# Input tiles of another layout between the first weight loads, and a quarter of the last norm's columns on GpSimd, in a two-layer decoder trunk

## The chip, the cores and the metric

The kernel runs on one core of a Trainium2 chip. A core has a matrix engine (TensorE, PE in the profile; its weight loads are PEld), VectorE (DVE), ScalarE (ACT), GpSimd (POOL) and SyncE (SP), which here issues most DMAs. The metric is the device time of one execution in microseconds (us), as the median of several runs.

## The reference

Two layers of a decoder trunk on 256 tokens of 1024 channels, all in 32-bit floats. Each layer is a half-step SwiGLU with a layer norm, three token mixers (gated DeltaNet, sliding-window attention, cross-attention to a memory) whose outputs are gated and projected, a layer norm, and a second half-step SwiGLU with a layer norm:

```python
def hybrid_layer(x, ...):
    h = layer_norm(ALPHA * x + 0.5 * swiglu(x, ffn1_w_gu, ffn1_w_down), ln_g[0], ln_b[0])
    ...
    h = layer_norm(ALPHA * h + merged @ w_out, ln_g[1], ln_b[1])
    return layer_norm(ALPHA * h + 0.5 * swiglu(h, ffn2_w_gu, ffn2_w_down), ln_g[2], ln_b[2])
```

What matters here is the first product, `x @ ffn1_w_gu` of layer 0, with which the kernel starts, and the last layer norm of layer 1, with which it ends.

## The kernel before

**Products.** A 32-bit factor is split into a high part, rounded to the matrix engine's reduced type, and a low part, the rest. `split` (line 121) does this with one cast on ACT and one subtraction on DVE. A product is then three matmuls (`mm3`): high by high, high by low, low by high.

**Weights.** All weights lie in DRAM in one stream `wst`, in the order of use. `unit` (lines 104 to 119) takes the next piece, normally 128 partitions by 1024 columns (512 KB): SP loads it into a tile `raw` (4 buffers), `split` makes `whi` and `wlo` (5 buffers each). With `cuts=2` it does so in two halves of 512 columns, each with its own DMA, cast and subtraction.

**The start.** The input is needed with channels on partitions. `xT` in DRAM is the plain transpose, 1024 channels by 256 tokens; `xload` (line 1047) loads 256 channels of it as a tile `t` of 128 partitions by 2 rows of 256 tokens (1 KB each, 256 KB in all), and splits it into `hT`. `Ffn.__init__` calls `xload(q)` and `unit` in turn for q = 0 to 3, the first unit in halves. So four x tiles and four weight units alternate on SP's queue; then follow the constants `cs` (488 KB, with the identity matrix for the transposes) and the further weights. `Ffn.both` (line 328) multiplies: for each k of 128 channels and each of two blocks of 128 tokens three matmuls of 512 columns, 48 in all, 12 for each weight unit. PE's order is fixed by the scheduler when the kernel is built; at the first k of a whole unit it places the two products with `whi` of both token blocks ahead of the first with `wlo`.

**The rest.** Then come the other gate and up columns, the down projection, the mixers and so on, for two layers. SP's queue keeps its order; a weight load waits until its `raw` buffer is free. DMAs from SP use eight completion semaphores in turn, so each waits for the one eight places ahead.

**The end.** The last down projection is ordered so that token block 1 ends last, its last 512 columns in two pieces of 256. `Post.__call__` calls `layernorm` (line 263) for each token block: add the residual (line 409), statistics (272, 275), the root on ACT (279), its reciprocal with one correction step on DVE (280 to 283), and for each half c of 512 columns two operations on DVE: `(y - mean) * g` (286) and `y * rs + b` (287). `fin` stores each half with a DMA from SP (416). GpSimd does nothing in this stretch.

Of the kernel before, what the change touches and what calls it, by code (L numbers as in the profile page):

```python
# [14 lines left out]
ALU = mybir.AluOpType  # L15
AX = mybir.AxisListType

P = 128
D = 1024
S = 256  # L20
# [3 lines left out]
KD = D // P  # L24
# [14 lines left out]
def tile_trunk(ctx, tc, x, xT, mem, memT_, wst, lnp, memln, cvw, rows, cst, out):  # L39
# [36 lines left out]
    def load(dst, src):  # L76

        tc.keep_in_program_order(nc.sync.dma_start(dst, src))
# [22 lines left out]

    pos, newest = [0], []

    def unit(w=U, dst=None, cuts=1, behind=None):
        ahead = tc.high_priority(offset=AHEAD) if pos[0] >= 8 * P * U else nullcontext()
        raw = T(praw, [P, U], "raw")
        src = wst[pos[0]:pos[0] + P * w].rearrange("(p w) -> p w", p=P)
        pos[0] += P * w
        (ph, th), (pl, tl) = dst or ((phi, "whi"), (plo, "wlo"))
        with ahead:  # L110
            hi = T(ph, [P, U], th, F32R)
            lo = T(pl, [P, U], tl, F32R)
            for i in range(cuts):
                c = slice(i * w // cuts, (i + 1) * w // cuts)
                nc.sync.dma_start(raw[:, c], src[:, c])
                with tc.issue_after(behind) if behind else nullcontext():
                    newest[:] = split(hi[:, c], lo[:, c], raw[:, c])
        return hi, lo
# [141 lines left out]
            nc.vector.tensor_tensor(t, t, v, op=ALU.mult)  # L260
            nc.vector.scalar_tensor_tensor(y, t, 1.5, y, op0=ALU.add, op1=ALU.mult)

    def layernorm(y, gB, bB, eps, src=None, fin=None, sizes=(512, 512)):
        n = min(sizes)
        st = T(p3, [P, 4, 6], "bnst")[:, :D // n, :]
        done = at_ = 0
        for j, size in enumerate(sizes):
            if src:
                src(j, slice(at_, at_ + size))
            at_ += size  # L270
            while done < at_:
                nc.vector.bn_stats(st[:, done // n, :], y[:, done:done + n])
                done += n
        mv = T(p3, [P, 2], "bnmv")
        nc.vector.bn_aggr(mv, st)
        rs = T(p3, [P, 1], "rstd")
        rt = T(p3, [P, 1], "rst")

        nc.scalar.activation(rs, mv[:, 1:2], AF.Sqrt, bias=epsc[:, eps:eps + 1])
        nc.vector.reciprocal(rs, rs)  # L280
        nc.vector.scalar_tensor_tensor(rt, mv[:, 1:2], epsc[:, eps:eps + 1], rs, op0=ALU.add, op1=ALU.mult)
        nc.vector.scalar_tensor_tensor(rt, rt, -0.5, rs, op0=ALU.mult, op1=ALU.mult)
        nc.vector.scalar_tensor_tensor(rs, rt, 1.5, rs, op0=ALU.add, op1=ALU.mult)
        for c in range(2):
            cc = slice(c * 512, (c + 1) * 512)
            nc.vector.scalar_tensor_tensor(y[:, cc], y[:, cc], mv[:, 0:1], gB[:, cc], op0=ALU.subtract, op1=ALU.mult)
            ins = nc.vector.scalar_tensor_tensor(y[:, cc], y[:, cc], rs, bB[:, cc], op0=ALU.mult, op1=ALU.add)
            if fin:
                fin(c)
        return ins.ins  # L290
# [9 lines left out]
    class Ffn:  # L300
        def __init__(self, before=None):
            self.units = []
            for q in range(KD // 2):
                if before:
                    before(q)
                self.units.append(unit(cuts=2 if before and q == 0 else 1))
            self.hu, self.bank, self.due = {}, {}, []

        def h(self, i):
# [76 lines left out]
    class Post:  # L386
# [12 lines left out]
        def __call__(self, tb, outs):  # L399
            if tb == 0:  # L400
                self.gb = gb(*self.aps)
                self.hT = None if self.last else new_hT()
            y = hres[tb]

            def put(q):
                return self.hT[0][:, q * 4:q * 4 + 4, :], self.hT[1][:, q * 4:q * 4 + 4, :]

            def src(j, c):
                nc.vector.scalar_tensor_tensor(y[:, c], outs[tb][j], 0.5 / ALPHA, y[:, c], op0=ALU.mult, op1=ALU.add)

            turns = []

            def fin(c):
                if self.last:
                    cc = slice(c * 512, (c + 1) * 512)
                    nc.sync.dma_start(out[tb * P:(tb + 1) * P, cc], y[:, cc])
                elif tb == 0:

                    turns.append(lambda: to_T(put, tb, y, c))
                else:  # L420
                    to_T(put, tb, y, c)

            self.end = layernorm(y, *self.gb, 1, src, fin, [o.shape[-1] for o in outs[tb]])
            return turns

    def begin(nxt, hT):
# [615 lines left out]


    hT = new_hT()
    xv = xT.rearrange("(k p) t -> p k t", p=P)

    def xload(q):
        raw = T(p2, [P, 2, S], "t2", bufs=4)
        load(raw, xv[:, q * 2:q * 2 + 2, :])
        split(hT[0][:, q * 2:q * 2 + 2, :], hT[1][:, q * 2:q * 2 + 2, :], raw)  # L1050


    idle = T(p2, [P, 512], "pp")
# [2 lines left out]
    for _ in range(2):  # L1056
        nc.tensor.matmul(ps, idle[:, 0:P], idle, start=True, stop=True)
    f1 = Ffn(xload)
    load(cs, cst)
    f1.both(hT)  # L1060
    hres = [pc.tile([P, D], F32, name=f"h{tb}") for tb in range(2)]

    def xres(tb):
        load(hres[tb], x[tb * P:(tb + 1) * P, :])
# [6 lines left out]
    for l in range(NL):  # L1071
        mT = []
        mid = memory_T(mT, l)
        if l == 0:

            more = {4: lambda *a: xres(0), 6: lambda *a: xres(1), 8: lambda *a: small()}
        post = Post(lnp[l, 0, 0], lnp[l, 0, 1])
        f1.rest(hT, 4, [((pu, "u0"), (pu, "u1")), ((pu, "u2"), (pu, "u3"))], post, mid, ends, {} if l else more)
# [102 lines left out]
```

## Time and profile before

| what | value |
|---|---|
| median of 3 runs | 1279.35 us (1277.74 to 1280.58) |
| profiled execution, its own time | 1280.75 us |
| span of that execution | 1279.0 us |
| granted TensorE clock, mean | 0.998 |
| PE busy | 1263.0 us (99%) |
| DVE busy | 866.5 us (68%) |
| ACT busy | 660.6 us (52%) |
| POOL busy | 210.6 us (16%) |
| DMA, mean | 204 GB/s |
| PE's share of the chain that ended last | 89% |

The profile comes from one execution. The span goes from the first to the last instruction; the execution's own time is 1.75 us more. Busy time is the time in which an engine works on at least one instruction. The chain that ended last is followed back from the last instruction, at each step to what released it.

### The profile page before, as it was taken

The numbers are of one execution on the slowest core, as the hardware profiler recorded it, in microseconds if no ns is written. First come the engines' busy times: TensorE is split into PE (matmuls) and PEld (weight loads), VectorE is DVE, ScalarE is ACT, GpSimd is POOL, SyncE is SP. The second block draws the span as 40 slices with busy tenths as digits, with TensorE's granted clock in tenths as the row PEclk, the third lists the DMA queues.
The fourth block names the chain that finished last, engine by engine and source line by source line (L and its number), as shares of the span: only waits on it lengthen the run. The fifth ranks groups of instructions, "written<-read, shape, count | busy, mean of one in ns | idle before, by whom it ended". The sixth has DMA issues, their size and how long they took to land.

```text
span 1279.0 us, 18765 instructions
## 1 busy us (share of the span) xinstructions
PE 1263.0 (99%) x6948; PEld 1073.8 (84%) x6948; DVE 866.5 (68%) x1271; ACT 660.6 (52%) x980; POOL 210.6 (16%) x365
## 2 busy tenths in 40 slices
PE   9999999999999999999999999999999999999997
PEld 6888889999878788888888888899987787888886
DVE  5788576886647776665776665759767388766655
ACT  6556444655664534444354554456656654444441
POOL 0232100002311202221012220010033102122200
PEclk9999999999999999999999999999999999999999
DMA  8988764655534728776667876556463256577762
GB/s 285 315 269 278 254 210 161 206 176 129 170 116 148 259 97 265 244 239 220 224 204 243 256 253 223 173 187 209 152 163 136 97 191 221 167 246 244 237 225 82
DMA packets 77499, 261.40 MB, mean 204 GB/s; under 512 B 11904, under 2 KB 13056, under 8 KB 77408
## 3 DMA queue, kind: packets, MB, share of 16 engines
q1 hardware_dynamic: 66320, 232.53, 55.2%
q0 software_dynamic: 11088, 27.68, 8.0%
q8 instruction: 54, 0.88, 0.3%
q14 instruction: 37, 0.30, 0.1%
HBM read 246.40 MB, written 13.76 MB: 203 GB/s over the span
## 4 chain that ended last, share of the span: by engine, by line
PE 89%; DMA 4%; DVE 3%; issue 2%; POOL 1%; ACT 1%; SPq 0%; DVEq 0%; ACTq 0%; POOLq 0%
PE acc L130 79%; PE at L130 3%; PE sm L130 3%; DMA raw<-in_wst_dram 2%; DVE wlo L121 2%; PE sm L133 1%; DMA w<-dr 1%; PE acc L323 1%; PE acc L324 1%; PE acc L326 1%; ACT whi L121 1%; PE at L133 1%; POOL t L797 1%; POOL l L788 0%; POOL t L798 0%
## 5 line engine op out<-in xcount | busy, mean ns | idle before, releaser
L121 DVE TENSOR_TENSOR wlo<-raw,whi 128x1024 fp32r<-128x1024 f32 (+2 forms) x403 | 489.3, 1222 | 282.1 <-ACT whi L121 280.2
L121 ACT CAST whi<-raw 128x1024 fp32r<-128x1024 f32 (+2 forms) x403 | 413.4, 1033 | 401.8 <-PE acc L130 321.4
L130 PE MATMUL acc<-whi,hT 128*128 128x512 f32 (+1 forms) x1824 | 563.2, 386 | 0.7 <-ACT whi L121 0.6
L130 PEld LDWEIGHTS acc<-whi,hT 128*128 128x128 f32 x1824 | 340.5, 188 | 70.3 <-ACT whi L121 3.0
L130 PE MATMUL acc<-wlo,hT 128*128 128x512 f32 (+1 forms) x912 | 350.7, 385 | 0.8 <-DVE wlo L121 0.8
L130 PE MATMUL acc<-whi,u 128*128 128x512 f32 x784 | 249.0, 392 | 0.0
L130 PEld LDWEIGHTS acc<-wlo,hT 128*128 128x128 f32 x912 | 171.6, 188 | 33.8 <-DVE wlo L121 1.7
L130 PEld LDWEIGHTS acc<-whi,u 128*128 128x128 f32 x784 | 147.3, 188 | 30.6
L130 PE MATMUL acc<-wlo,u 128*128 128x512 f32 x392 | 152.8, 390 | 0.0
L353 POOL DMA_DIRECT2D tr<-t x176 | 96.2, 553 | 304.3 <-DVE t L347 295.1
L130 PE MATMUL acc<-hT,whi 128*128 128x256 f32 x672 | 122.3, 284 | 0.0
L130 PEld LDWEIGHTS acc<-hT,whi 128*128 128x128 f32 x672 | 104.7, 192 | 0.0
L130 PE MATMUL acc<-hT,wlo 128*128 128x256 f32 x336 | 95.2, 283 | 0.0
L130 PEld LDWEIGHTS acc<-wlo,u 128*128 128x128 f32 x392 | 73.7, 188 | 14.7
L130 PEld LDWEIGHTS acc<-hT,wlo 128*128 128x128 f32 x336 | 64.4, 192 | 0.0
L354 POOL DMA_DIRECT2D pt<-tr x44 | 25.0, 568 | 194.7 <-DMA tr<-t 148.5
L344 ACT ACTIVATE t<-acc 128x256 f32<-128x256 f32 x88 | 33.5, 380 | 38.3 <-PE acc L130 38.2
L990 POOL TENSOR_TENSOR u<-u,gt 128x512 f32<-128x512 f32 x16 | 24.4, 1529 | 131.0 <-DVE gt L988 131.0
L345 DVE TENSOR_TENSOR t<-t,acc 128x256 f32<-128x256 f32 x88 | 36.7, 417 | 9.1 <-ACT t L344 4.7
L121 DVE TENSOR_TENSOR u<-pt,u 128x512 fp32r<-128x512 f32 x44 | 28.9, 657 | 11.8 <-ACT u L121 11.8
L121 DVE TENSOR_TENSOR u<-raw,u 128x1024 fp32r<-128x1024 f32 x24 | 30.9, 1290 | 7.4 <-ACT u L121 7.4
L130 PE MATMUL acc<-whi,w 128*128 128x512 f32 x96 | 31.8, 402 | 3.6 <-DVE w L121 3.5
(236 smaller groups left out, 1204.3 us busy)
## 6 DMA issues: line engine op xcount, KB each, us to landing
raw<-in_wst_dram SPq DMA_DIRECT2D x409, 512.0 KB, 4.4
tr<-t POOLq DMA_DIRECT2D x176, 64.0 KB, 3.8
pt<-tr POOLq DMA_DIRECT2D x44, 256.0 KB, 5.0
raw<-in_wst_dram SPq DMA_DIRECT2D x16, 324.0 KB, 2.9
gB<-in_lnp_dram SPq DMA_DIRECT2D x6, 512.0 KB, 5.9
bB<-in_lnp_dram SPq DMA_DIRECT2D x6, 512.0 KB, 5.9
w<-dr POOLq DMA_DIRECT2D x4, 512.0 KB, 11.5
t<-in_xT_dram SPq DMA_DIRECT2D x4, 256.0 KB, 6.1
```

The lines of the kernel that those rows point to most:

```text
L121: return nc.scalar.copy(hi, src).ins, nc.vector.tensor_tensor(lo, src, hi.bitcast(F32), op=ALU.subtract).ins
L130: return pe(nc.tensor.matmul(*a, **k))
L133: return pe(nc.tensor.transpose(*a))
L323: nc.tensor.matmul(ps, hT[0][:, k, ts], hi[:, c], start=k == 0, stop=False)
L324: nc.tensor.matmul(ps, hT[0][:, k, ts], lo[:, c], start=False, stop=False)
L326: nc.tensor.matmul(ps, hT[1][:, k, ts], hi[:, c], start=False, stop=k == KD - 1)
L344: act = nc.scalar.activation(t[:, :, tb, :], g, AF.Silu).ins
L345: ins = nc.vector.tensor_tensor(t[:, :, tb, :], t[:, :, tb, :], u, op=ALU.mult).ins
L353: nc.gpsimd.dma_start(d[:, :, q].rearrange("b c x -> c b x"), z[32 * q:32 * q + 32].rearrange("c (b x) -> c b x", b=4))
L354: back = nc.gpsimd.dma_start(y, d.rearrange("b c q x -> (b c) (q x)")).ins
L797: nc.gpsimd.tensor_tensor(pr16[:, :, 0:n], ab[j // 8][:, j % 8, :, j + 1:16], y16[:, :, j:j + 1].to_broadcast([P, 8, n]), op=ALU.mult)
L990: nc.gpsimd.tensor_tensor(mg[tb][:, js], mg[tb][:, js], gt[tb][:, js], op=ALU.add)
```

## The change

Four things change, in one edit.

1. `xT` is laid out in DRAM as the partitions read it: 128 partitions by 8 by 256, so that two k of a partition lie next to each other.
2. `xload(a, n)` loads n k from a on. The first two k come as two tiles of 128 KB, the second of them between the two halves of the first weight unit (`amid`); the other three tiles hold two k as before. The second weight unit comes in halves, too.
3. The load of `cs` goes from behind the first four units to a point in the middle of the first SwiGLU (`mid[2]`).
4. In the last norm, for token block 1 alone (`ends`), GpSimd takes columns 768 to 1023 with four operations: subtract the mean, multiply by g, multiply by the reciprocal root, add b. DVE's second half shrinks to 256 columns. The last store waits for both engines.

```diff
-    def unit(w=U, dst=None, cuts=1, behind=None):
+    def unit(w=U, dst=None, cuts=1, behind=None, amid=None):
...
             for i in range(cuts):
+                if amid and i:
+                    amid()
                 c = slice(i * w // cuts, (i + 1) * w // cuts)
                 nc.sync.dma_start(raw[:, c], src[:, c])
...
         nc.scalar.activation(rs, mv[:, 1:2], AF.Sqrt, bias=epsc[:, eps:eps + 1])
+        if ends:
+
+            y3, g3, b3 = (t[:, 768:] for t in (y, gB, bB))
+            nc.gpsimd.tensor_scalar(y3, y3, mv[:, 0:1], None, ALU.subtract)
+            nc.gpsimd.tensor_tensor(y3, y3, g3, op=ALU.mult)
         nc.vector.reciprocal(rs, rs)
...
+        if ends:
+            nc.gpsimd.tensor_scalar(y3, y3, rs, None, ALU.mult)
+            nc.gpsimd.tensor_tensor(y3, y3, b3, op=ALU.add)
         for c in range(2):
-            cc = slice(c * 512, (c + 1) * 512)
+            cc = slice(c * 512, (768 if ends else 1024) if c else 512)
...
-                    before(q)
-                self.units.append(unit(cuts=2 if before and q == 0 else 1))
+                    before(2 * q, 1 if q == 0 else 2)
+                self.units.append(unit(cuts=2 if before and q < 2 else 1, amid=(lambda: before(1, 1)) if before and q == 0 else None))
...
-    def xload(q):
-        raw = T(p2, [P, 2, S], "t2", bufs=4)
-        load(raw, xv[:, q * 2:q * 2 + 2, :])
-        split(hT[0][:, q * 2:q * 2 + 2, :], hT[1][:, q * 2:q * 2 + 2, :], raw)
+    def xload(a, n):
+        raw = T(p2, [P, n, S], "t2", bufs=4)
+        load(raw, xT[:, a:a + n, :])
+        split(hT[0][:, a:a + n, :], hT[1][:, a:a + n, :], raw)
...
     f1 = Ffn(xload)
-    load(cs, cst)
     f1.both(hT)
...
+            mid[2] = lambda: load(cs, cst)
```

How the instructions stand on the engines shows in three places. The first is SP's queue at the start. `t` is an x tile, `raw` the tile of a weight unit (`raw_114` is w0, the next three are w1, w2 and w3), `cs` the constants. Before:

```order
L78 DMA t_5_110<-in_xT_dram 128x2x256
L115 DMA raw_114<-in_wst_dram 128x512 x2
L78 DMA t_9_123<-in_xT_dram 128x2x256
L115 DMA raw_127<-in_wst_dram 128x1024
L78 DMA t_13_133<-in_xT_dram 128x2x256
L115 DMA raw_137<-in_wst_dram 128x1024
L78 DMA t_17_143<-in_xT_dram 128x2x256
L115 DMA raw_147<-in_wst_dram 128x1024
L78 DMA cs<-in_cst_dram 128x976
L115 DMA raw_222<-in_wst_dram 128x1024
```

The same queue in the changed kernel:

```order
L78 DMA t_5_110<-in_xT_dram 128x256
L117 DMA raw_114<-in_wst_dram 128x512
L78 DMA t_9_120<-in_xT_dram 128x256
L117 DMA raw_114<-in_wst_dram 128x512
L78 DMA t_10_127<-in_xT_dram 128x512
L117 DMA raw_131<-in_wst_dram 128x512 x2
L78 DMA t_14_140<-in_xT_dram 128x512
L117 DMA raw_144<-in_wst_dram 128x1024
L78 DMA t_18_150<-in_xT_dram 128x512
L117 DMA raw_154<-in_wst_dram 128x1024
L117 DMA raw_228<-in_wst_dram 128x1024
```

Two DMAs more stand ahead of the third weight unit (`raw_137` before, `raw_144` now), the second unit has two, and `cs` is gone from here; it stands behind twelve further weight loads.

The second place is DVE at the start, where the low parts of x (`hT`) and of the weights (`wlo`) are made, before:

```order
L121 TENSOR_TENSOR hT_104<-t_5_110,hT_104 128x2x256
L121 TENSOR_TENSOR wlo_116<-raw_114,whi_115 128x512 x2
L121 TENSOR_TENSOR hT_104<-t_9_123,hT_104 128x2x256
L121 TENSOR_TENSOR wlo_129<-raw_127,whi_128 128x1024
L121 TENSOR_TENSOR hT_104<-t_13_133,hT_104 128x2x256
L121 TENSOR_TENSOR wlo_139<-raw_137,whi_138 128x1024
```

and in the changed kernel:

```order
L123 TENSOR_TENSOR hT_104<-t_5_110,hT_104 128x256
L123 TENSOR_TENSOR wlo_116<-raw_114,whi_115 128x512
L123 TENSOR_TENSOR hT_104<-t_9_120,hT_104 128x256
L123 TENSOR_TENSOR wlo_116<-raw_114,whi_115 128x512
L123 TENSOR_TENSOR hT_104<-t_10_127,hT_104 128x2x256
L123 TENSOR_TENSOR wlo_133<-raw_131,whi_132 128x512 x2
L123 TENSOR_TENSOR hT_104<-t_14_140,hT_104 128x2x256
L123 TENSOR_TENSOR wlo_146<-raw_144,whi_145 128x1024
```

The second unit's subtraction is now two of 512 columns; the third unit's is one of 1024, as before.

The third place is the last norm, token block 1: DVE before, from the end of the statistics on (`h` is the output, `rstd` the reciprocal root):

```order
L275 BN_AGGR bnmv_11824<-bnst_11816 128x2
L286 SCALAR_TENSOR_TENSOR h_219<-h_219,bnmv_11824,gB_11738 128x512
L280 RECIPROCAL rstd_11826<-rstd_11826 128x1
L286 SCALAR_TENSOR_TENSOR h_219<-h_219,bnmv_11824,gB_11738 128x512
L281 SCALAR_TENSOR_TENSOR rst_11827<-bnmv_11824,epsc,rstd_11826 128x1
L282 SCALAR_TENSOR_TENSOR rst_11827<-rst_11827,rstd_11826 128x1
L283 SCALAR_TENSOR_TENSOR rstd_11826<-rst_11827,rstd_11826 128x1
L287 SCALAR_TENSOR_TENSOR h_219<-h_219,rstd_11826,bB_11739 128x512 x2
```

and DVE in the changed kernel:

```order
L277 BN_AGGR bnmv_11831<-bnst_11823 128x2
L296 SCALAR_TENSOR_TENSOR h_225<-h_225,bnmv_11831,gB_11745 128x512
L287 RECIPROCAL rstd_11833<-rstd_11833 128x1
L296 SCALAR_TENSOR_TENSOR h_225<-h_225,bnmv_11831,gB_11745 128x256
L288 SCALAR_TENSOR_TENSOR rst_11834<-bnmv_11831,epsc,rstd_11833 128x1
L289 SCALAR_TENSOR_TENSOR rst_11834<-rst_11834,rstd_11833 128x1
L290 SCALAR_TENSOR_TENSOR rstd_11833<-rst_11834,rstd_11833 128x1
L297 SCALAR_TENSOR_TENSOR h_225<-h_225,rstd_11833,bB_11746 128x512
L297 SCALAR_TENSOR_TENSOR h_225<-h_225,rstd_11833,bB_11746 128x256
```

with this at the end of GpSimd's queue in the changed kernel, behind the last DMAs of the SwiGLU, where nothing stood before:

```order
L364 DMA pt_11363<-tr_11364 128x512
L285 TENSOR_SCALAR h_225<-h_225,bnmv_11831 128x256
L286 TENSOR_TENSOR h_225<-h_225,gB_11745 128x256
L292 TENSOR_SCALAR h_225<-h_225,rstd_11833 128x256
L293 TENSOR_TENSOR h_225<-h_225,bB_11746 128x256
L1186 UNCONDITIONAL_BRANCH
```

DVE keeps all its steps, two of them with half the columns; GpSimd has four steps beside them.

## Rows read from the trace of the kernel before

**Rows 1.** Chain of waits, whole span: start us, length us, engine, tile, line.

```profile
2.67 6.39 DMA raw<-in_wst_dram
9.09 1.05 ACT whi L121
10.16 1.24 DVE wlo L121
11.44 174.10 PE acc L130 x766
```

**Rows 2.** Timeline of SP's queue: start us, us, engine, line, operation, tile<-source, count.

```profile
2.67 0.47 SPq L115 DMA_DIRECT2D raw<-in_wst_dram  x1
...
3.66 0.47 SPq L115 DMA_DIRECT2D raw<-in_wst_dram  x1
...
6.05 0.44 SPq L78 DMA_DIRECT2D cs<-in_cst_dram  x1
```

**Rows 3.** DMA issues at 2.67 and 3.66 us: tiles, queue, count, KB, us to landing.

```profile
raw<-in_wst_dram SPq DMA_DIRECT2D x1, 512.0 KB, 6.4
...
raw<-in_wst_dram SPq DMA_DIRECT2D x1, 512.0 KB, 7.4
```

**Rows 4.** Timeline of the start, ACT and DVE: as rows 2, then idle and releaser.

```profile
4.71 0.62 ACT L121 CAST whi<-raw 128x512 fp32r<-128x512 f32 x1 [0.47 <-DMA raw<-in_wst_dram]
5.36 0.69 DVE L121 TENSOR_TENSOR wlo<-raw,whi 128x512 fp32r<-128x512 f32 x1 [0.39 <-ACT whi L121]
...
12.21 1.23 DVE L121 TENSOR_TENSOR wlo<-raw,whi 128x1024 fp32r<-128x1024 f32 x1 [0.22 <-ACT whi L121]
```

**Rows 5.** ACT at 38.5 us (timeline); transposes: ns min/median/max, first and last start.

```profile
38.52 1.05 ACT L121 CAST whi<-raw 128x1024 fp32r<-128x1024 f32 x1 [1.59 <-PE acc L130]
...
L133 PE MATMUL sm<-cs,h x80: 270/273/328, 188.3 to 1095.1; 128*128 128x128 f32 x80
```

**Rows 6.** Timeline of the last norm on DVE.

```profile
1271.85 0.26 DVE L275 BATCH_NORM_AGGREGATE bnmv<-bnst 128x2 f32<-128x24 f32 x1
...
1272.15 0.75 DVE L286 SCALAR_TENSOR_TENSOR h<-h,bnmv,gB 128x512 f32<-128x512 f32 x1
...
1272.89 0.73 DVE L286 SCALAR_TENSOR_TENSOR h<-h,bnmv,gB 128x512 f32<-128x512 f32 x1
1273.55 0.21 DVE L281 SCALAR_TENSOR_TENSOR rst<-bnmv,epsc,rstd 128x1 f32<-128x1 f32 x1
...
1274.18 1.41 DVE L287 SCALAR_TENSOR_TENSOR h<-h,rstd,bB 128x512 f32<-128x512 f32 x2
```

**Rows 7.** Groups by line and shape: Pool, then DVE: count, busy us, mean ns, idle before.

```profile
L799 POOL TENSOR_TENSOR w<-t,cs 128x256 f32<-128x256 f32 x2 | 1.5, 740 | 0.2
...
L793 POOL COPY t<-cs 128x128 f32<-128x128 f32 x2 | 0.6, 290 | 0.1
...
L409 DVE SCALAR_TENSOR_TENSOR h<-at,h 128x256 f32<-128x256 f32 x12 | 5.0, 416 | 3.5 <-PE at L130 3.5
```

**Rows 8.** Pool and DVE side by side (timeline, two places); Pool's small copies (min/median/max ns).

```profile
435.80 1.30 POOL L990 TENSOR_TENSOR u<-u,gt 128x512 f32<-128x512 f32 x1 [2.96 <-DVE gt L988]
...
436.18 2.00 DVE L121 TENSOR_TENSOR wlo<-raw,whi 128x1024 fp32r<-128x1024 f32 x1
...
959.48 0.16 DVE L738 TENSOR_TENSOR mx<-mx,rw 128x4 f32<-128x4 f32 x1
...
959.66 0.38 POOL L797 TENSOR_TENSOR t<-w,t 128x104 f32<-128x104 f32 x1
...
959.68 0.38 DVE L739 TENSOR_TENSOR sk<-rw,mx 128x4 f32<-128x4 f32 x1
...
L868 POOL COPY w<-w x16: 280/286/1310, 355.2 to 991.5; 32x128 f32<-32x128 f32 x16
```

**Rows 9.** Pool's configuration step (ns, first and last start) and first two-input operation (timeline).

```profile
L530 POOLq MODIFY_POOL_CONFIG  x2: 5/5/5, 213.9 to 214.0; - x2
...
225.57 1.28 POOL L530 TENSOR_TENSOR u<-u,rw 128x512 f32<-128x512 f32 x1 [11.57 <-ACT u L527]
```

More of the change, by code (lines that the diff above doesn't have):

```diff
@@ L261, in rsqrt, with layernorm @@
             nc.vector.scalar_tensor_tensor(y, t, 1.5, y, op0=ALU.add, op1=ALU.mult)
-    def layernorm(y, gB, bB, eps, src=None, fin=None, sizes=(512, 512)):
+    def layernorm(y, gB, bB, eps, src=None, fin=None, sizes=(512, 512), ends=False):
         n = min(sizes)
@@ L421, in fin @@
                     to_T(put, tb, y, c)
-            self.end = layernorm(y, *self.gb, 1, src, fin, [o.shape[-1] for o in outs[tb]])
+            self.end = layernorm(y, *self.gb, 1, src, fin, [o.shape[-1] for o in outs[tb]], self.last and tb)
             return turns
@@ L1044, in tile_trunk @@
     hT = new_hT()
-    xv = xT.rearrange("(k p) t -> p k t", p=P)
-    def xload(q):
-        raw = T(p2, [P, 2, S], "t2", bufs=4)
-        load(raw, xv[:, q * 2:q * 2 + 2, :])
-        split(hT[0][:, q * 2:q * 2 + 2, :], hT[1][:, q * 2:q * 2 + 2, :], raw)
+    def xload(a, n):
+        raw = T(p2, [P, n, S], "t2", bufs=4)
+        load(raw, xT[:, a:a + n, :])
+        split(hT[0][:, a:a + n, :], hT[1][:, a:a + n, :], raw)
     idle = T(p2, [P, 512], "pp")
@@ L1159 @@
         "x": i["x"][0],
-        "xT": np.ascontiguousarray(i["x"][0].T),
+        "xT": np.ascontiguousarray(i["x"][0].T.reshape(KD, P, S).transpose(1, 0, 2)),
         "mem": i["mem"][0],
```

## The prediction

> **What bounds the kernel now.** I read the chain of waits first, over the whole span. It is TensorE nearly throughout: after a short start the chain runs on PE alone, 766 matmul pieces in 174.10 us from 11.44 us on [rows 1]. That is 0.2273 us for each matmul, and since nothing interrupts them, a microsecond saved before 11.44 us is a microsecond saved at the end, as long as what comes after moves along. Two places are not PE: the first 11.44 us, where the chain is the load of a weight unit, its cast on ACT and its subtraction on VectorE (DVE), and the last few microseconds, where the final layernorm runs on DVE after the last matmul [rows 6]. The change touches just these two, and moves the load of the constants.
>
> Call the weight units w0, w1, w2, w3 (512 KB each; w0 comes in two halves). Each unit feeds 12 matmuls in this first stage: two row blocks times three products for each of two k. Of a unit not split up, PE takes two products with the high part first and then needs the low part. A wait that ends at time t with n matmuls done puts PE at a **start line** of t - 0.2273 n; the latest of these lines sets the rest. Before, the last wait is for the low part of w1, at 11.44 us, with 12 + 2 = 14 matmuls done: line 11.44 - 3.18 = 8.26 us.
>
> **The start, part by part.** The queue of SP issues x and weights in turn. w1 is issued at 2.67 and w2 at 3.66 [rows 2], and they land 6.4 and 7.4 us later [rows 3], at 9.07 and 11.06. From there a whole unit needs a cast of 1.05 us [rows 1] and then a subtraction of 1.23 us [rows 4] before its low part is usable; two halves need 0.62 and 0.69 each, one behind the other on two engines [rows 4].
>
> *w1 in halves.* Taken as though both halves landed only at 9.07: cast 9.09 to 9.71, subtraction to 10.42, PE at 10.46 with 14 done: line 7.28. The second half follows one cast later and is ready near 11.1 with 18 + 1 done: line 6.8. So w1 no longer decides.
>
> *What is late next: w2.* It is still whole. Its subtraction before ran from 12.21 for 1.23 us [rows 4], so PE could have it at 13.48 (0.04 us on, as with w1). Before, PE got there at 8.26 + 26 x 0.2273 = 14.17 and did not wait. Now it would get there at 7.28 + 5.91 = 13.19 and waits 0.29 us: line 13.48 - 5.91 = 7.57. For w3, w2 followed w1 by 1.99 us with an x tile between them, and w3 follows w2 in the same way, so it lands near 13.05, is usable near 15.47, with 36 + 1 done: line 7.06, no wait. Gain 8.26 - 7.57 = **0.69 us**.
>
> *The x tiles.* The first tile is half as large and its twin goes between the halves of w0; the bytes ahead of w1 and w2 stay the same (x of the same k, same weights), so I let w2 land when it did. That is the choice on which the term rests. Upper end: two more DMAs stand in front of w2, and if each pushes it by one issue of 0.47 us [rows 2], w2 is usable at 14.42, line 8.51: a loss of 0.25 us. Lower end: w2 lands 0.3 us or more earlier, because of fewer and longer packets, and w1 decides: a gain of 0.98 us. I take 0.69, since the row of w2 is a row of that transfer itself. The fifth x tile reuses the buffer of the first; its issue waits for DVE's subtraction of the first tile, long done by then, and only w3 is queued behind it.
>
> *The constants* (one issue of 0.44 us at 6.05 [rows 2], 488 KB) leave the queue ahead of the fifth unit and go behind the sixteenth, at some 33 us. Their first reader is a transpose at 188.3 us [rows 5]. Where they now stand, they push weight loads back by about their own transfer. By 38.52 us ACT waits for PE to free a cast buffer and not for a load [rows 5], so the loads are ahead there; cost nothing. If that cover were gone, the price would be at most the transfer, some 1.3 us by the 1.99 us in which 768 KB landed between w1 and w2.
>
> **The tail, part by part.** In the last norm the statistics end at 1271.85 + 0.26. DVE then runs two column halves of subtract-and-scale (0.75, 0.73), three small steps for the reciprocal root (1273.55 to 1274.18) and two halves of scale-and-add (1.41 together): the end is at 1275.59 [rows 6]. Now columns 768 to 1023 go to GpSimd (Pool) in four operations, and DVE's second halves shrink to 256 columns, 0.41 us each by a vector operation of that width [rows 7]. Pool's two-input operation on 256 columns took 0.74 us; its one-input operation is not in the trace; the copy of 128 columns took 0.29 [rows 7], so I take 0.45, nearer to the copy, with ends of 0.29 and 0.74.
>
> *If the engines ran freely*, DVE would have the root 0.3 us earlier, at 1273.85, and finish near 1274.95; Pool, from the root, would need 0.45 + 0.74 and two hand-overs, ending near 1275.2: a gain of 0.4 us.
>
> *They do not run freely.* In [rows 8], Pool's two-input operation held 435.80 to 437.10, and DVE's subtraction behind it took 2.00 us where 1.23 is usual: it ended 1.08 us after Pool. A tiny DVE operation on two SBUF tensors took 0.38 us next to 0.16 for its neighbour, and ended with Pool's. Pool's own copies, usually 0.286, took up to 1.310. An operation of Pool and a two-tensor operation of DVE thus exclude each other, whole instruction by whole instruction; the waiting one saves some 0.14 us of its start-up (1.23 - 1.08 and 0.38 - 0.36 as against 0.16). Every DVE step in this tail but the reciprocal reads two SBUF tensors. So add all of it in a row: 0.75 + 0.45 + 0.41 + 0.74 + 0.63 (small steps) + 0.75 + 0.45 + 0.41 + 0.74 = 5.33, less seven hand-overs of 0.14 = 4.35. From 1272.15 that ends at 1276.50: **0.91 us later** than 1275.59. Worst: no saving at hand-overs and one-input operations of 0.74: 5.91, a loss of 2.47. The rows show this for plain two-tensor operations, while the tail has the form with a scalar besides. The Trainium skill ("GPSIMD Engine Reference", 1. Specifications) says that Pool shares its SBUF interfaces with VectorE and contends with VectorE instructions that have two SBUF inputs; by that rule the scalar form counts too, and the sum is +0.91, without it -0.4.
>
> The new waits: Pool waits for the statistics and the root, with nothing but its own operations behind; SP's last store now waits for Pool as well, with nothing behind.
>
> **Sum.** -0.69 + 0.91 = +0.22 us. The profiled execution took 1280.75 us (span 1279.0), so 1280.97 in its terms; it lies 1.40 above the median of 1279.35, so the predicted median is 1279.57, say **1279.6**.
>
> **The rivals.**
> - *No exclusion in the tail:* -0.69 - 0.4 = -1.1, 1278.2. For it: no scalar form beside Pool in the trace. Against: even tiny operations are held.
> - *The start gives nothing* (two more DMAs ahead of w2, the change does not do what it sets out to): +0.25 + 0.91 = +1.2, 1280.5. For it: the landing times grow with each DMA issued. Against: bytes, not DMAs, fill the queue by then.
> - *The start gives the most and the exclusion half of its price:* -0.98 + 0.45 = -0.5, 1278.8.
> - *Slower by a first call on Pool.* Pool has not run this one-input operation before; if it must first fetch its code, the whole tail hangs on it. Before, a configuration step stands at 213.9 to 214.0 and Pool's first two-input operation at 225.57 [rows 9]; up to 11.57 us could hide there. If the first operation lasts X, Pool ends some X + 2.2 after 1272.2, X - 1.2 later than before; it decides from X = 4.4 us, where the total passes 2.56 us. With all 11.57: +10.4 - 0.7, 1289. Against: that first operation itself took 1.28 us, and both copies 0.290. The Trainium skill ("GPSIMD Engine Reference", 2.1 Instruction dispatch) gives a first call to a freshly loaded kernel an invisible load of about 6 us; by that figure an estimate of +4.1, 1283.5; no run here shows one.
>
> **How the numbers follow.** Chances: forecast 0.58; start gives nothing 0.20; no exclusion 0.11; the half-and-most case 0.06; first call 0.05. A measurement can tell about 0.2% from no change, 2.56 us; below 1276.8 counts as faster, above 1281.9 as slower. All cases but the last lie inside. Scatter of the runs (1277.74 to 1280.58) takes 0.03 to the faster side and 0.02 to the slower one: faster 0.03, same 0.90, slower 0.07. The cases reach from 1277.9 (-0.98 - 0.4) to 1282.1 (+0.25 + 2.47); with the scatter below and little chance at the top, the range is 1277.4 to 1281.8.
>
> **What would show it.** Right at the start: PE's last wait ends near 13.5 on the low part of w2, and no wait follows. Wrong: it ends on w1, or w2 lands a microsecond off 11.06. Right in the tail: DVE's small steps or last halves are drawn out to the ends of Pool's operations, and the last vector work ends 4.3 us after the statistics. Wrong: DVE ends by 1275 in the old time, or Pool's first operation lasts microseconds.

## The result, and the profile after

The changed kernel took 1281.70 us (median; 1280.36 to 1286.98), the kernel before beside it 1279.63: ratio 1.0019, interval 1.0012 to 1.0026, some 2.4 us more (1.5 to 3.3). A second set of runs gave 1.0013 (1.0002 to 1.0024). Forecast were 1279.6 and +0.22 us against 1279.35. 1281.7 lies just inside the range, but nearly all of the way to its slow end, and it is a change that a measurement can tell, though less than 0.2%.

The chain of waits of the changed kernel at the start (start us, length us, what), where [rows 1] ended on w1:

```profile
4.47 7.56 DMA raw<-in_wst_dram
12.05 1.06 ACT whi L123
13.13 1.24 DVE wlo L123
14.41 171.39 PE acc L132 x754
```

The wait that ends last is now that for w2, as forecast: 26 matmuls are done, 754 follow without a break. But w2 landed at 12.03 (4.47 + 7.56), not at 11.06, so the start line is 14.41 - 5.91 = 8.50 us, 0.24 later than before, where 7.57 was forecast.

SP's queue (start us, us, what, count) and ACT (then idle and its releaser), for [rows 2] and [rows 4]:

```profile
3.04 0.91 SPq L117 DMA_DIRECT2D raw<-in_wst_dram  x2
...
4.47 0.91 SPq L117 DMA_DIRECT2D raw<-in_wst_dram  x1
...
32.45 0.43 SPq L78 DMA_DIRECT2D cs<-in_cst_dram  x1
```

```profile
9.10 1.30 ACT L123 CAST whi<-raw 128x512 fp32r<-128x512 f32 x2 [0.48 <-DMA raw<-in_wst_dram]
...
12.05 1.05 ACT L123 CAST whi<-raw 128x1024 fp32r<-128x1024 f32 x1 [0.65 <-DMA raw<-in_wst_dram]
...
38.78 1.05 ACT L123 CAST whi<-raw 128x1024 fp32r<-128x1024 f32 x1 [1.67 <-PE acc L132]
```

The two halves of w1 are cast one behind the other at 9.10 and w2 at 12.05. The table cs goes out at 32.45, and at 38.78 ACT waits for TensorE as in [rows 5]: that move costs nothing in this trace.

DVE and Pool in the last norm (timeline), for [rows 6]:

```profile
1273.50 0.26 DVE L277 BATCH_NORM_AGGREGATE bnmv<-bnst 128x2 f32<-128x24 f32 x1
...
1273.80 0.75 DVE L296 SCALAR_TENSOR_TENSOR h<-h,bnmv,gB 128x512 f32<-128x512 f32 x1
1273.95 1.41 POOL L285 TENSOR_SCALAR h<-h,bnmv 128x256 f32<-128x256 f32 x1 [47.66 <-issue]
...
1274.54 0.63 DVE L296 SCALAR_TENSOR_TENSOR h<-h,bnmv,gB 128x256 f32<-128x256 f32 x1
1275.09 0.21 DVE L288 SCALAR_TENSOR_TENSOR rst<-bnmv,epsc,rstd 128x1 f32<-128x1 f32 x1
1275.33 0.16 DVE L289 SCALAR_TENSOR_TENSOR rst<-rst,rstd 128x1 f32<-128x1 f32 x1
1275.44 0.72 POOL L286 TENSOR_TENSOR h<-h,gB 128x256 f32<-128x256 f32 x1
1275.53 0.65 DVE L290 SCALAR_TENSOR_TENSOR rstd<-rst,rstd 128x1 f32<-128x1 f32 x1
1276.21 1.37 DVE L297 SCALAR_TENSOR_TENSOR h<-h,rstd,bB 128x512 f32<-128x512 f32 x2
1276.35 1.41 POOL L292 TENSOR_SCALAR h<-h,rstd 128x256 f32<-128x256 f32 x1 [0.19 <-DVE rstd L290]
1277.85 0.72 POOL L293 TENSOR_TENSOR h<-h,bB 128x256 f32<-128x256 f32 x1
```

Vector work ends at 1277.85 + 0.72 = 1278.57. From the end of the statistics (1273.80, the start of the next operation) that is 4.77 us; before it was 1275.59 - 1272.15 = 3.44. So the tail lost 1.33 us where +0.91 was forecast.

Between start and tail no instruction was changed, yet the two traces also part there. The last matmul (timeline of TensorE, first of after, then of before):

```profile
1272.27 0.28 PE L132 MATMUL at<-whi,u 128*128 128x256 f32 x1
```

```profile
1270.62 0.28 PE L130 MATMUL at<-whi,u 128*128 128x256 f32 x1
```

It ends 1.65 us later, 0.24 of it from the start. The other 1.41 come mainly from two waits in the middle that a second execution of the same kernel does not have ("The middle", below). The last 0.18 us of the difference in span (2.8) run the other way, behind the vector work: 3.23 against 3.41 us.

### The profile page after: what moved, and what is told of

Same layout as the page of the kernel before. It is cut to its first block, busy times and chain, and to the rows that moved or that the text cites. A ratio compares the mean times of both kernels' runs of the same rounds, so it can differ in the third digit from the quotient of the medians.

```text
span 1281.8 us, 18783 instructions
## 1 busy us (share of the span) xinstructions
PE 1264.6 (99%) x6948; PEld 1074.8 (84%) x6948; DVE 867.5 (68%) x1273; ACT 660.7 (52%) x982; POOL 214.0 (17%) x369
## 4 chain that ended last, share of the span: by engine, by line
PE 87%; DMA 6%; DVE 3%; ACT 1%; issue 1%; POOL 0%; SPq 0%; POOLq 0%; DVEq 0%; ACTq 0%
PE acc L132 76%; DMA raw<-in_wst_dram 4%; PE at L132 4%; PE sm L132 3%; DVE wlo L123 2%; PE sm L135 1%; ACT whi L123 1%; DMA tr<-t 1%; PE acc L333 1%; PE acc L334 1%; PE acc L336 1%; DMA pt<-tr 1%; PE at L135 1%; DVE u L123 0%; DMA bB<-in_lnp_dram 0%
## 5 line engine op out<-in xcount | busy, mean ns | idle before, releaser
L123 ACT CAST u<-pt 128x512 fp32r<-128x512 f32 x44 | 26.9, 610 | 18.4 <-DMA pt<-tr 18.4
```

The source lines that it names most:

```text
L123: return nc.scalar.copy(hi, src).ins, nc.vector.tensor_tensor(lo, src, hi.bitcast(F32), op=ALU.subtract).ins
```

## The experiments

My theory after the two traces: the start's loss is real, since w2 lands late, and the tail's is the contention of Pool and DVE with a dearer one-input operation. Its rivals: the landing of w2 was chance; 1.41 us is the one-input operation's own price; the loss arises in the middle. Each expectation names its theories for its own kernel.

### Each part alone

tail_alone is the kernel before with the last norm's edit, start_alone the changed kernel without it:

```
-            self.end = layernorm(y, *self.gb, 1, src, fin, [...], self.last and tb)
+            self.end = layernorm(y, *self.gb, 1, src, fin, [...])
```

> The kernel before with only the change of the last norm. Theory 1 (the two ends carry the loss, the middle is chance): the time from the end of the last statistics to the end of the vector work goes from 3.44 us to 4.77, as in the changed kernel (1273.80 to 1278.57), with GpSimd's one-input operations at 1.41 us; the run is 1.0 to 1.3 us slower, and the start line of TensorE stays at 8.26. Rival (most of the loss sits in the start and in what it shifts in the middle): this kernel is within 0.6 us of the kernel before.

> The changed kernel without GpSimd's part of the last norm (VectorE does all 1024 columns again). Theory 1: w2 lands near 12.0, the start line is 8.5, so 0.25 us slower than before, and nothing else that is systematic. Rival: the constants' load and the shifted order of DMA semaphores cost something in the middle, as the shift of 0.26 to 1.65 us between 130 and 1100 us in the profile of the changed kernel suggests: then this kernel is 1.0 us or more slower, with such a shift again at the same places.

tail_alone: ratio 1.0011 (0.9999 to 1.0023). Its norm takes the same 4.77 us, 1269.04 to 1273.81. start_alone: ratio 0.9997 (0.9980 to 1.0013), too wide for its part; w2 landed at 12.39, line 8.86, and the norm took 3.44 us. What I had not counted on is the start of tail_alone, which issues what the kernel before issues:

```profile
2.66 5.33 DMA raw<-in_wst_dram
...
10.37 174.10 PE acc L130 x766
```

w1 landed at 7.99 instead of 9.06, line 10.37 - 3.18 = 7.19 instead of 8.26. The one profile of before was a late draw. Its start appeared in four kernels in all: 8.26, 7.19, and in the two below 8.04 and 7.06, mean 7.64.

### The price of Pool's operations by themselves

pool_price runs them on scratch tiles at the start, where DVE has nothing to do:

```
...
+    nc.gpsimd.memset(sa, 1.0)
+    nc.gpsimd.tensor_scalar(sb, sa, zero, None, ALU.subtract)
+    nc.gpsimd.tensor_scalar(sa, sb, zero, None, ALU.mult)
+    nc.gpsimd.tensor_tensor(sb, sb, sa, op=ALU.add)
+    nc.gpsimd.tensor_scalar(sb[:, 0:128], sa[:, 0:128], zero, None, ALU.mult)
+    nc.gpsimd.tensor_copy(sa, sb)
...
+    f1 = Ffn(xload)
```

> The kernel before, with GpSimd operations on two scratch tiles at the start, where VectorE is idle until about 4.2 us: one-input with a scalar per partition on 256 columns (twice), two-input on 256, one-input on 128, copy of 256, two-input with a broadcast column. What they cost alone. Theory A (exclusion): the one-input operation alone takes about 0.9 us, and the 1.41 of the last norm is 0.5 of waiting for VectorE's first half. Theory B: it takes 1.41 alone, so it is simply dear, and does not wait. Two-input 0.74 in both, copy 0.4. If a first call costs something, the first of the twins is longer than the second.

Pool's timeline:

```profile
1.19 0.93 POOL L1060 TENSOR_SCALAR scr<-scr,zero 128x256 f32<-128x256 f32 x1
2.21 0.94 POOL L1061 TENSOR_SCALAR scr<-scr,zero 128x256 f32<-128x256 f32 x1
3.23 0.73 POOL L1062 TENSOR_TENSOR scr<-scr,scr 128x256 f32<-128x256 f32 x1
4.06 0.61 POOL L1063 TENSOR_SCALAR scr<-scr,zero 128x128 f32<-128x128 f32 x1
4.73 0.63 POOL L1064 COPY scr<-scr 128x256 f32<-128x256 f32 x1
```

The one-input operation with a scalar per partition takes 0.93 us on 256 columns, more than the two-input one (0.73). On 128 columns it takes 0.61, so the copy of 0.29 [rows 7] was no guide to it. The first one lasts as long as the second: no first call is paid here.

tail_quiet is tail_alone without DVE's first pass (subtract and gain) over its three quarters:

```
+            if not ends:
                 nc.vector.scalar_tensor_tensor(y[:, cc], y[:, cc], mv[:, 0:1], gB[:, cc], op0=ALU.subtract, op1=ALU.mult)
```

> The kernel before with GpSimd's quarter of the last norm alone, and VectorE's first pass over its three quarters of the columns (subtract the mean, times the gain) left out, so that this part of the output lacks it. Theory A (GpSimd and VectorE shut each other out, and GpSimd's one-input op takes 0.93 us by itself): GpSimd's first op takes 0.9 to 1.1 us instead of 1.41, its two-input op 0.72, and VectorE's three small ops after the reciprocal are held only while GpSimd's two run. The second one-input op, beside which VectorE still runs its second pass, takes 1.4 again. Rival B (1.41 is what this op costs on these operands, whoever runs beside it): the first op takes 1.41 as before.

```profile
1270.06 0.94 POOL L283 TENSOR_SCALAR h<-h,bnmv 128x256 f32<-128x256 f32 x1 [49.34 <-issue]
...
1270.70 0.16 DVE L287 SCALAR_TENSOR_TENSOR rst<-rst,rstd 128x1 f32<-128x1 f32 x1
1270.89 0.16 DVE L288 SCALAR_TENSOR_TENSOR rstd<-rst,rstd 128x1 f32<-128x1 f32 x1
...
1271.09 1.88 DVE L296 SCALAR_TENSOR_TENSOR h<-h,rstd,bB 128x512 f32<-128x512 f32 x2
1271.91 1.25 POOL L290 TENSOR_SCALAR h<-h,rstd 128x256 f32<-128x256 f32 x1
```

With DVE's large operations gone the same instruction on the same operands takes 0.94, not 1.41; beside the second pass the next one takes 1.25, where 1.4 was expected. Rival B (1.41 is its own price) falls. Theory A holds in its main point, but not as whole-instruction exclusion: the [128x1] steps of DVE at 1270.70 and 1270.89 were expected to be held while it runs, and take their usual 0.16 us beside Pool's one-input operation. How much of the 0.47 us more in the changed kernel is waiting for DVE's first half, which ends 0.60 us after Pool's operation begins, and how much is slower running, these traces don't tell. Beside the two-input one, such a step took 0.65 (1275.53 in after) and ended with it.

### What delays w2

halves_alone is the kernel before with one edit, halves_again the same timed:

```
-                self.units.append(unit(cuts=2 if before and q == 0 else 1))
+                self.units.append(unit(cuts=2 if before and q < 2 else 1))
```

> The kernel before with the second weight unit in halves and nothing else: one DMA more ahead of w2. Theory (each DMA ahead of w2 puts it off by one issue, about 0.47 us): w2 lands near 11.5, is usable near 13.95, start line 8.0, 0.25 us earlier than before. Rival (w2 is put off by the small x tiles or by the other layout, not by the number of DMAs): w2 lands at 11.06, start line 7.57.

> The kernel before with both pieces of the first weights' second tile (w1) cut in halves and nothing else, a second time, now timed. Theory 1 (the landing of w2 scatters by a microsecond or more from execution to execution, and nothing else moves): w2 lands between 10.4 and 11.4, the stretch of 754 products then starts 26 products in, and its line (its start less 26 x 0.2273) lies between 6.9 and 7.9 against 8.26 before; the time is 0.4 to 1.3 us under the time before, ratio 0.9990 to 0.9997, which the interval may not tell from 1. Theory 2 (the 10.47 of the first look was the rule and not chance): landing within 0.2 of 10.47, line 6.9 to 7.1, ratio 0.9988 to 0.9992. Theory 3 (the middle of the program gives any start back): ratio within 0.0002 of 1 whatever the line.

w2 landed at 10.47 and 10.37, earlier than either theory of halves_alone had it, lines 6.94 and 6.84; ratio 0.9988 (0.9976 to 0.9999), nearest to theory 2. So the halves do what they are for, and the changed kernel loses that somewhere else in its start. Two edits were left: the layout in DRAM, and the single columns of x. halves_layout puts the layout into halves_alone; start_old_layout takes it out of start_alone:

```
-        load(raw, xv[:, q * 2:q * 2 + 2, :])
+        load(raw, xT[:, q * 2:q * 2 + 2, :])
...
-        "xT": np.ascontiguousarray(i["x"][0].T),
+        "xT": np.ascontiguousarray(i["x"][0].T.reshape(KD, P, S).transpose(1, 0, 2)),
```

> The halves of w1 as in halves_alone, and the input in DRAM in the order in which partitions read it; tiles of x still four pairs, table cs still where it was before. Theory L (the new layout, whose rows are 2 KB and not 1 KB long, is what makes the queue move less between 5 and 10 us in the changed kernel, 210 to 290 GB/s against 310 to 410): w2 is issued at 4.14 and lands at 11.6 to 12.2 instead of 10.47, so the line of the 754 products is 8.1 to 8.7. Theory N (the two further DMAs for single columns of x do it): w2 lands as in halves_alone, 10.3 to 10.9, line 6.8 to 7.4. Theory C (chance): anything from 10.4 to 12.4, with no reason for a lower rate of the queue between 5 and 10 us.

> The whole start of the changed kernel (tiles of x of one, one, two, two and two, between halves of w0, halves of w1, cs moved), but the input in DRAM in the old order, and no GpSimd in the last norm. Theory L (the layout lowers the rate): w2, issued at 4.49, lands at 10.6 to 11.2 instead of the 12.05 and 12.39 of the two kernels with the new layout, line 7.1 to 7.7. Theory N (number and size of the DMAs): w2 lands at 11.9 to 12.5 as with the new layout, line 8.4 to 9.0. Theory C (chance): anything from 10.8 to 12.8.

> halves_layout a second time, now timed: halves of w1, a row of 2 KB out of every 8 KB for a tile of x. Theory L (the layout of the change costs the queue about 1.4 us by the landing of w2): w2 lands at 11.5 to 12.3, line 8.0 to 8.8; against the mean of the four starts of before's instructions seen so far (8.26, 7.19, 8.04, 7.06, mean 7.64) that is +0.4 to +1.2 us, ratio 1.0003 to 1.0009. Theory C (chance): w2 at 10.4 to 11.4, line 6.9 to 7.9, ratio 0.9990 to 1.0000.

> The whole start of the change with the old layout, a second look. Theory L: w2 lands at 10.6 to 11.3 as in the first (10.91), line 7.1 to 7.8, between halves alone (10.37, 10.47) and the changed kernel (12.05, 12.39). Theory C (chance): above 11.5.

The chain of waits of halves_again, then of halves_layout, then of start_old_again:

```profile
4.15 6.22 DMA raw<-in_wst_dram
...
12.75 171.39 PE acc L130 x754
```

```profile
4.04 7.80 DMA raw<-in_wst_dram
...
14.22 171.41 PE acc L130 x754
```

```profile
4.54 6.11 DMA raw<-in_wst_dram
...
13.03 171.41 PE acc L132 x754
```

The layout decides. Put into the halves of w1, it moves w2 from 10.47 and 10.37 to 11.84 and 11.72 (lines 8.31 and 8.20); taken out of the whole start of the change, it moves w2 from 12.03 and 12.39 to 10.91 and 10.65 (7.38 and 7.12). layout_again's ratio is 1.0003 (0.9994 to 1.0011), where halves without the layout had 0.9988. A delay already stands in the first load, with nothing queued ahead of it. The tile's view of x gives the times from issue to landing, first for halves_alone, then for halves_layout:

```profile
DMA to landing us min/median/max: 2.8/5.1/6.6
```

```profile
DMA to landing us min/median/max: 3.7/5.8/7.9
```

The least is that of the first pair, 2.8 us against 3.7. And from 2 to 4 us (busy time of PE, PEld, DVE, ACT, Pool, then clock, DMA share, GB/s) the queue moves 267 GB/s in halves_again (291 in halves_alone) against 157 in halves_layout:

```profile
2.00:4.00 2.00, 2.00 (x3) 0.69 (x3) 0.00 (x0) 1.16 (x3) 0.00 (x0) 1.00 0.75 267
```

```profile
2.00:4.00 2.00, 2.00 (x3) 0.69 (x3) 0.00 (x0) 1.16 (x3) 0.00 (x0) 1.00 0.62 157
```

But this first delay is not what reaches w2. From 4 to 6 us halves_layout moves 375 GB/s against 291 in halves_again, and the casts of w1's two halves start at 7.55 and right behind it, against 7.20 and 8.26 there: level. The loss comes back at the third tile of x, just ahead of w2. Its cast on ACT, in halves_again and in halves_layout (then idle and releaser):

```profile
9.07 0.62 ACT L121 CAST hT<-t 128x512 fp32r<-128x512 f32 x1 [0.20 <-DMA t<-in_xT_dram]
```

```profile
10.57 0.62 ACT L121 CAST hT<-t 128x512 fp32r<-128x512 f32 x1 [1.75 <-DMA t<-in_xT_dram]
```

layout_again has 10.36 there and halves_alone 9.19. From this tile on w2 is late by as much.

The layout does two things: a row is 2 KB and not 1 KB, and the rows of a tile lie 8 KB apart. halves_tiled keeps the 2 KB and puts the rows of one tile one behind the other:

```
-        load(raw, xT[:, q * 2:q * 2 + 2, :])
+        load(raw, xT[q])
...
+        "xT": np.ascontiguousarray(i["x"][0].T.reshape(KD // 2, 2, P, S).transpose(0, 2, 1, 3)),
```

> As halves_layout (halves of w1, each tile of x read as 128 rows of 2 KB), but in DRAM the rows of one tile stand one behind the other, 256 KB in one piece, where halves_layout and the changed kernel take a row of 2 KB out of every 8 KB. Theory S (the step of 8 KB between the rows of a tile is what slows the queue): w2 lands as with the old layout, at 10.2 to 10.9, line of the 754 products 6.7 to 7.4, ratio to before 0.9988 to 0.9996. Theory R (rows of 2 KB instead of 1 KB slow it): w2 lands at 11.5 to 12.3, line 8.0 to 8.8, ratio 1.0000 to 1.0010. Theory C (11.84, 12.05 and 12.39 were chance): anywhere between.

```profile
4.02 6.17 DMA raw<-in_wst_dram
...
12.57 171.38 PE acc L130 x754
```

```profile
DMA to landing us min/median/max: 2.8/4.9/6.4
```

w2 lands at 10.19, line 6.66, the first pair 2.8 us after its issue; ratio 0.9988 (0.9979 to 0.9997). Its third tile of x is cast at 8.92. In this start the step between the rows slows the loads, not their length (theory S), by one trace with the rows in one piece and by the times: 0.9988 without the step, 1.0003 with it.

### The change with the step mended

after_again is the changed kernel once more; after_tiled has each tile of x in one piece; start_tiled is that without Pool's part:

```
-        load(raw, xT[:, a:a + n, :])
+        load(raw, xT[a * P:(a + n) * P, :].rearrange("(p k) t -> p k t", p=P))
...
+        "xT": np.concatenate([... for a, b in ((0, 1), (1, 2), (2, 4), (4, 6), (6, 8))]),
```

> The changed kernel a second time. If the layout and the tail are the two causes: w2 lands at 11.7 to 12.4 again, line of the 754 products 8.1 to 8.9 (8.50 and 8.86 so far), against the mean 7.64 of the four starts of before's instructions that is +0.5 to +1.2 us; the tail takes 4.77 us from the end of the aggregation to the end of the vector work, against 3.44; together +1.7 to +2.4 us, ratio 1.0013 to 1.0019. If the start was chance: line 7.0 to 8.0, ratio 1.0005 to 1.0011.

> The changed kernel with one thing mended: the rows of each tile of x stand one behind the other in DRAM, in place of a row out of every 8 KB. If that step is what cost the start: w2 lands at 10.3 to 11.0, line 6.8 to 7.5, that is -0.1 to -0.8 us to the mean start of before; GpSimd's tail stays at 4.77 us, +1.15 to +1.33; together +0.3 to +1.2 us, ratio 1.0002 to 1.0010. If the two single columns of x cost as much as the step: w2 above 11.5, ratio 1.0012 or more.

> after_tiled without GpSimd in the last norm. Line 6.8 to 7.5 as there, the tail 3.44 us as before: -0.1 to -0.8 us to before, ratio 0.9993 to 0.9999, and 1.15 to 1.33 us under after_tiled. Rival: the tail's loss is given back in what follows the vector work, then it stands level with after_tiled.

The chain of waits of after_again, then of after_tiled:

```profile
4.47 7.10 DMA raw<-in_wst_dram
...
13.95 171.43 PE acc L132 x754
```

```profile
4.47 6.63 DMA raw<-in_wst_dram
...
13.49 171.39 PE acc L132 x754
```

Ratios: after_again 1.0013 (1.0002 to 1.0024), after_tiled 1.0002 (0.9990 to 1.0014), start_tiled 0.9990 (0.9979 to 1.0002). The order is as expected, and the last two are 0.0012 apart, 1.5 us, as the tail's 1.33 wants, although their intervals overlap. The norm took 4.77 us in after_again and after_tiled and 3.44 in start_tiled. The starts were not as expected. after_again's w2 landed at 11.57, line 8.04, just earlier than the 11.7 and 8.1 that I had as the least. With each tile in one piece w2 landed at 11.10 and 11.61, lines 7.58 and 8.08 where I had 6.8 to 7.5; 11.61 is no earlier than after_again, and above the 11.5 of after_tiled's rival, though the ratios are not where that rival has them. The first tile has its 2.1 us from issue to landing back (2.1 with the old layout, 2.5 in the changed kernel), but later loads don't keep that lead; why is open. So in the whole start mending the step gives back 0.64 us of w2's landing (means 12.00 and 11.36), where the old layout gives back 1.22, and the rest is not explained.

All starts together (landing = start plus length of the DMA in the chain, without the chain's DMA row the start of the cast; line = start of TensorE's stretch less 0.2273 us for each matmul done):

| start | x in DRAM | w2 landed, us | line, us |
|---|---|---|---|
| before: w1 whole | old | 11.1, 10.0, 10.9, 9.9 | 8.26, 7.19, 8.04, 7.06 (set by w1) |
| w1 in halves | old | 10.47, 10.37 | 6.94, 6.84 |
| w1 in halves | 8 KB step | 11.84, 11.72 | 8.31, 8.20 |
| w1 in halves | tile in one piece | 10.19 | 6.66 |
| whole start | old | 10.91, 10.65 | 7.38, 7.12 |
| whole start (after) | 8 KB step | 12.03, 12.39, 11.57 | 8.50, 8.86, 8.04 |
| whole start | tile in one piece | 11.10, 11.61 | 7.58, 8.08 |

### A version that beats both

halves_three also cuts w2:

```
-                self.units.append(unit(cuts=2 if before and q < 2 else 1))
+                self.units.append(unit(cuts=2 if before and q < 3 else 1))
```

> The kernel before with w1 and w2 in halves (x, its layout and cs untouched). If the landing of w2 as a whole and the 2.36 us of split behind it set the start (line 6.84 and 6.94 in the two looks at halves of w1 alone), halving w2 takes that away and w3 is next: it lands 0.47 later than the 12.37 to 12.52 there, 12.8 to 13.0, its split ends 2.36 later, 38 products in, line 6.4 to 6.8, a gain of 0.1 to 0.5 us over halves of w1 and of 0.9 to 1.3 us over the mean start of before; ratio 0.9990 to 0.9993. Rival: the further DMA delays all that lands behind it by more than 0.47, line 7 or more, ratio 0.9995 to 1.0002.

Its chain of waits:

```profile
1.74 4.45 DMA raw<-in_wst_dram
...
6.21 6.93 DMA raw<-in_wst_dram
```

Ratio 0.9990 (0.9981 to 0.9999). w2 no longer decides, but w3, issued only at 6.21, landed at 13.14 (its cast starts at 13.16) and TensorE waited for it until 15.52, 38 matmuls in: line 15.52 - 8.64 = 6.88, no better than halves of w1 alone. The rival's mechanism is right, its size smaller than it said. The chain shows what held w3's issue: the second half of w0, issued at 1.74 and landed at 6.19. It stands eight DMAs ahead of w3, since one DMA more has moved w3 a place back in the turn of the eight semaphores; with w1 alone in halves w3 was issued at 5.22. Halves of w1 alone, with the old layout or with each tile in one piece, thus beat before (both 0.9988, some 1.5 us, of which their lines of 6.66 to 6.94 against 7.64 account for 0.7 to 1.0) and the changed kernel. Which of the two is better was not told apart.

### The middle

From the start line to the end of the last matmul before took 1270.90 - 8.26 = 1262.64 us and after 1272.55 - 8.50 = 1264.05. The same in the other profiles runs from 1260.60 (tail_alone, 1267.79 - 7.19) to 1266.74 (start_old_layout, 1274.12 - 7.38), with 1260.69 and 1262.45 for two executions of one and the same kernel (halves_again, halves_alone). after_again has 1262.41, below before.

Where the 1.41 us arise can be seen in the chains of before and after, by the starts of the same stretches of TensorE. The stretch of 352 matmuls starts at 197.28 and 197.54, one of 24 at 404.01 and 404.26: up to there the change is 0.25 us behind, what its start lost, and the move of the constants to 32.45 us has cost nothing. A stretch of 46 starts at 441.88 and 442.58, 0.70 behind, and the one of 732 at 651.84 and 654.26, 2.42 behind; from 1101.96 and 1103.61 on it is 1.65. The two waits of after behind this (timeline of TensorE and DVE):

```profile
432.87 0.73 PE L132 MATMUL acc<-whi,w 128*128 128x512 f32 x2 [1.65 <-DVE w L123]
...
637.70 1.42 DVE L297 SCALAR_TENSOR_TENSOR h<-h,rstd,bB 128x512 f32<-128x512 f32 x2 [1.79 <-DMA bB<-in_lnp_dram]
638.50 0.66 PE L135 MATMUL sm<-cs,h 128*128 128x128 f32 x4 [1.19 <-DVE h L297]
```

At the first, TensorE stood still for 1.65 us in one piece (1.12 in before at this place), and then its granted clock was 0.50, the lower level of 1.2 GHz, from 434 to 437 us; before's stayed at 1.00. At the second, a norm waited for its table bB, which SP issued at 631.68 and not at 627.65. after_again, with the same instructions, has neither: it issued bB at 627.4, and its stretch of 732 starts at 651.43. So the 1.41 us belong to that one execution, not to the change, and the rival falls. The two longest middles, start_old_layout and pool_price (1266.45), also have a stretch at 0.50, behind pauses of TensorE of 1.98 and 1.55 us.

## Why the prediction was wrong

- **What bounds the kernel, and which wait ends last**: right. The chain stands on w2 with 26 matmuls done, and the 754 behind it run without a wait.
- **The halves of w1**: right in mechanism. Alone they give lines of 6.94 and 6.84, where 7.57 was forecast, against a mean of 7.64.
- **"the bytes ahead of w1 and w2 stay the same ..., so I let w2 land when it did"**: this step failed. The bytes were the same, but the addresses were not. The new layout delays w2 by 11.78 - 10.42 = 1.36 us with halves alone and by 12.00 - 10.78 = 1.22 in the whole start (means). With halves alone that is the 8 KB step between rows, as the same rows in one piece land w2 at 10.19; in the whole start no more than 0.64 of it can be put down to the step, and the rest is open. The mean line of after is 8.47 against 7.64: +0.83 us in place of -0.69. The upper end that I gave (line 8.51) came out nearly to the figure, but for a wrong reason: it was put down to two DMAs more. With the old layout the whole start, which has those DMAs, lands w2 at 10.78 (mean), 0.36 us after halves alone and within the 9.9 to 11.1 of before. A lower end of "fewer and longer packets" had the right place and the wrong sign. That layout was the one edit whose price I never gave a row, and the rival "the start gives nothing" had 0.20.
- **One profile as the base**: before's line of 8.26 was the latest of four draws (7.06 to 8.26). A term of 0.69 us was worked out to hundredths from landings that move by more than that for the same instructions.
- **The constants**: right at nothing. The move was not tried alone, but after keeps its 0.25 us behind before from 197 to 404 us.
- **The tail**: right in sign, and in that Pool and DVE hold each other up, +1.33 instead of +0.91. Two things were off, in opposite directions. The one-input operation was taken at 0.45 (ends 0.29 and 0.74) and has 0.93; two of them add 0.96, so that the sum of 4.35 would have become 5.31. And the exclusion "whole instruction by whole instruction" does not hold for that operation: it grows to 1.41 and the 256 columns of DVE at 1274.54 to 0.63 instead of 0.41, but these begin and end within it, and the whole takes 4.77, not 5.31. The path at the end is Pool's: root at 1276.18, 0.38 us later after the statistics than before, then 2.39 us of Pool in place of 1.44 us of DVE. The Trainium skill ("GPSIMD Engine Reference", 1. Specifications) puts contention on DVE operations with two SBUF inputs; the traces agree, with 0.94 against 1.41 for the same operation, in the form with a scalar too.
- **The first call on Pool**: the rival falls, 0.93 and 0.94 for the first and second in pool_price, 0.94 for the first in the norm of tail_quiet.
- **The sum**: +0.83 and +1.33 make +2.2, against 2.4 (1.5 to 3.3) and 1.7 (0.3 to 3.1) measured. Forecast +0.22; the start is 1.52 of the miss (0.62 of it the late base, 0.90 the line of 8.47 where 7.57 was forecast) and the tail 0.42.

## What to carry to other kernels

When a change alters how a tile lies in DRAM, price the addresses and not just bytes and packets: try each tile in one piece in the order it is loaded, and follow the landing of every tile up to the one that is waited for: here the first load's delay was made up, and the third tile's was not. Moving part of a norm to Pool only pays if its own operations, priced alone and then beside DVE, are shorter than what they take off DVE; here Pool's quarter of the second pass took 1.41 + 0.72 us after the root, where DVE alone did all columns in 1.41. And before a term of tenths is built on one profile's landing times, look at more than one execution.

## What the hardware showed that I had not expected

- A load of 128 rows of 2 KB, 8 KB apart, as the first DMA of the program landed 3.7 us after its issue (halves_layout and layout_again), against 2.8 for the same rows in one piece and 2.7 to 3.3 for the old order of 1 KB rows. What in the memory does that is open. The Trainium skill ("DMA: Bandwidth & Descriptors", Latency and other measured facts) tells of a loss by row pitch in copies between HBM tensors, with the advice to pad the pitch or lay tiles out contiguously; its smallest pitch is 512 KiB, at 207 GB/s, close to the 214 that it calls full. The advice to lay tiles out contiguously agrees with halves_tiled (2.8 against 3.7); that a pitch of 8 KB costs something it does not say.
- Landing of w1 for identical instructions: 7.87 to 9.06 us.
- TensorE's granted clock in the profile of the changed kernel fell to 0.50 for about 3 us, right behind a pause of 1.65 us in the middle of the program.
- Pool's one-input operation with a scalar per partition (0.93 us on 256 columns) is dearer than its two-input one (0.73) and its copy (0.63).
